# A hybrid decoder block on one core: gates, branch projections and output projection by Strassen's scheme

## The chip, the cores and the metric

The kernel runs on one core of a Trainium2 chip. The metric is device time in microseconds for one execution; the kernel before took 1918.51 us as the median of three runs (1917.52 to 1919.49). A core has a matrix engine (TensorE, PE in the profile, with its weight loads as PEld), a vector engine (VectorE, DVE), an activation engine (ScalarE, ACT), a general engine (GpSimd, POOL) and an engine that here only issues transfers (SyncE, SP). Each engine takes its own queue in order, and waits on semaphores for the others.

## The reference, cut to what matters

One layer works on 1024 tokens and 16 meta tokens in front, with 1024 features. From the normalised stream `xn` one product gives the inputs of three token mixers and the gate logits; each mixer's result is projected, gated and summed, and one more product follows:

```python
xn = rms_norm(x, norm_pre)
proj = xn @ w_in                       # mixers' inputs, and 3 x 1024 gate logits
y_ssd, y_sc, y_dn = three mixers       # each tokens x 1024
branch = einsum("btnw,nwd->btnd", stack([y_ssd, y_sc, y_dn]), w_branch)
gates = sigmoid(gate_logits)           # tokens x 3 x 1024
merged = sum(gates * branch, over the three)
out = merged @ w_out
return x + rms_norm(out, norm_post)    # meta tokens dropped
```

So behind the mixers there are seven products of 1024 x 1024 by 1024 x 1024: three for the gates, three for the branches, one for the output.

## The kernel before

All products are float32 made of three products of rounded parts: a number is split into a high part (ScalarE casts it) and a low part (VectorE subtracts the high part from it), and high times high, high times low and low times high are added up in PSUM (`dense`, L157 to L159). A dense job is 128 output features: its weights come in one 512 KB transfer (`load_raw`, L127), are split (`split`, L135 and L136) one job ahead, and are multiplied with the stream, which stands split in SBUF (`xh`, `xl`), in groups of up to 512 tokens. A matmul of the tail thus has 128 x 128 weights and 512 columns.

The stream is normalised, transposed and split first. Then the mixers run, head by head: eight slots for the DeltaNet heads, eight for pairs of SSD heads. `weave` lays a mixer's small dependent steps between the matmuls of dense jobs: each step says how many columns of dense work it is worth waiting for, times a factor from the table `GAPS`. A DeltaNet slot has eight dense jobs: four of the next head and four of the short-convolution branch. The last SSD slot has three gate jobs (`early_gates`), whose results are parked in DRAM.

Behind the mixers (from `cp` on) the other 21 gate jobs and 24 branch jobs alternate (`gate_job`, `branch_job`). A branch's input is read back from DRAM and split beforehand (`y_tasks`, L974 to L981); the third branch is scaled at that point (L1007). A branch's results are multiplied by the gate straight from PSUM (L1039, L1041) and added to the sum `merged` (L1042). At the end `merged` and `w_out` are split and multiplied token block by token block (L1131 to L1133), and each token block is normalised, scaled, added to x (L1135 to L1149) and stored; the last one in three pieces (L1139, L1144).

The order in each queue is fixed at build time by a scheduler that follows the order of the code and the dependences. GpSimd makes masks and memsets and a few 128x512 sums (L692, L696) while the mixers run, and nothing after them.

Of the kernel before, what the change touches and what calls it, by code (L numbers as in the profile page):

```python
# [83 lines left out]
def hybrid_block(  # L84
# [419 lines left out]
    def dn_mix(h, tiles):  # L504
# [205 lines left out]
    def sc_jobs(t):  # L710
# [170 lines left out]
    def gate_col(b, d):  # L881
        return C_G + b * D + d * P

    def early_gates():
        """The first gates of the branch that comes first, parked in DRAM."""
        for d in range(PARKED):
            def go(w, d=d):
                gs = tmp(f"pg{d}")
                yield from act_job(gs, f"pg{d}", AF.Sigmoid)(w)
                DMA.dma_start(parked[d], gs[:, :SEQ])  # L890

            lazy(gate_col(ORDER[0], d), go)

# [15 lines left out]

    slot("dn", None, lambda: dn_jobs(0, dnt[0]))  # L910
    for h in range(DN_H):
        fs = [lambda h=h: sc_jobs(h)]
# [37 lines left out]
    wk.close()  # L950
    ab.__exit__(None, None, None)

# [1 line left out]
    cp = ctx.enter_context(tc.tile_pool(name="cp", bufs=1))  # L954
    ZERO = [(0, HALF), (HALF, HALF)]
    AHEAD = 3

    def slab(name, dt=F32):
        return cp.tile([P, SEQ], dt, name=name, tag="c", bufs=12)

    merged = [None] * KT
    order = [(b, (y_sd, y_sc, y_dn)[b]) for b in ORDER]
    yt = {}
    gates = {}

    halves = [slice(hf * HALF, (hf + 1) * HALF) for hf in range(2)]

    def staged(src, hi, lo, first=None):
        """Two tasks: fetch half a row block, and put its two exact parts in place."""
        box = {}  # L970

        def fetch():
            box["t"] = cp.tile([P, HALF], F32, tag="yr", name="yr", bufs=3)
            DMA.dma_start(box["t"], src)  # L974

        def put():
            t = box["t"]
            if first is not None:
                first(t)
            A.copy(hi(), t)  # L980
            V.tensor_tensor(lo(), t, hi().bitcast(F32), ALU.subtract)  # L981

        return fetch, put

    def pipelined(pairs, lead=2):
        f, p = [x[0] for x in pairs], [x[1] for x in pairs]
        for i in range(len(pairs) + lead):
            def step(i=i):
                if i >= lead:
                    p[i - lead]()  # L990
                if i < len(pairs):
                    f[i]()
            yield step
# [186 lines left out]
```

## Time and profile before

| | |
|---|---|
| median of the runs | 1918.51 us (1917.52 to 1919.49) |
| span of the profiled execution, first to last instruction | 1917.7 us |
| PE busy | 1892.8 us (99%) |
| DVE busy | 1060.5 us (55%) |
| ACT busy | 688.1 us (36%) |
| POOL busy | 161.8 us (8%) |
| first matmul of the parked gates | 1284.8 us |
| first matmul of the other gates | 1327.1 us |
| first matmul of the output projection | 1822.4 us |
| granted TensorE clock, mean | 0.997 |

The span is 0.8 us below the median of the runs. A row of a timeline gives the start of an instruction in microseconds from the span's start, its duration, engine, line and operation, what it writes and reads, and how long its engine sat idle before it. On PE the next matmul starts before the one in front has ended, so the pace is read from starts or from counts, not from durations.

### The profile page before, as it was taken

How to read it: one execution, taken by the hardware profiler on the slowest of the kernel's cores; microseconds unless marked ns; L12 is line 12 of the kernel's file. 1: busy time of each engine (PE TensorE's matmuls, PEld its weight loads, DVE VectorE, ACT ScalarE, POOL GpSimd, SP SyncE). 2: the span in 40 equal slices, each digit the busy share in tenths (PEclk: the TensorE clock that was granted, in tenths of full speed). 3: DMA queues.
4: the chain of work that ended last, by engine and by line, in shares of the span. 5: the costliest groups of instructions: out<-in, count | busy, mean ns of one | idle time of the engine just before them, and what ended most of it. 6: DMA issues, size and time to landing. Idle time of an engine off the chain costs nothing.

```text
span 1917.7 us, 27827 instructions
## 1 busy us (share of the span) xinstructions
PE 1892.8 (99%) x11475; PEld 1633.1 (85%) x11475; DVE 1060.5 (55%) x1748; ACT 688.1 (36%) x1248; POOL 161.8 (8%) x289
## 2 busy tenths in 40 slices
PE   6999999999999999999999999999999999999998
PEld 5988989889898898988989889888888888888887
DVE  5565666656666566665666788785323223622542
ACT  5543424334243342533425455464312211311231
POOL 2001001010010100101001111110000000000000
PEclk8999999999999999999999999999999999999999
DMA  5211111111211112111122123124413312411312
GB/s 150 58 34 56 44 53 48 45 56 45 62 39 45 56 45 67 34 45 56 45 67 78 56 89 100 56 78 150 130 44 87 100 44 72 135 47 56 116 66 88
DMA packets 163673, 131.40 MB, mean 69 GB/s; under 512 B 9329, under 2 KB 144686, under 8 KB 163546
## 3 DMA queue, kind: packets, MB, share of 16 engines
q1 hardware_dynamic: 162682, 126.74, 22.2%
q8 instruction: 90, 1.47, 0.3%
q10 hardware_dynamic: 720, 2.36, 0.3%
q0 software_dynamic: 144, 0.52, 0.1%
q14 instruction: 37, 0.30, 0.1%
HBM read 111.14 MB, written 18.46 MB: 68 GB/s over the span
## 4 chain that ended last, share of the span: by engine, by line
PE 94%; DVE 3%; ACT 1%; issue 1%; DMA 1%; POOL 0%; SPq 0%; DVEq 0%; POOLq 0%; ACTq 0%
PE b L158 5%; PE b L159 5%; PE b L157 5%; PE g L158 4%; PE g L159 4%; PE g L157 4%; PE po L1132 2%; PE po L1133 2%; PE po L1131 2%; PE pg L157 1%; PE pg L158 1%; PE pg L159 1%; DVE wl L136 0%; DMA gain<-in_norm_pre_dram 0%; PE sm L333 0%
## 5 line engine op out<-in xcount | busy, mean ns | idle before, releaser
L135 ACT CAST wh<-raw 128x1024 fp32r<-128x1024 f32 x132 | 138.7, 1051 | 369.0 <-PE b L158 190.9
L136 DVE TENSOR_TENSOR wl<-raw,wh 128x1024 fp32r<-128x1024 f32 x132 | 162.1, 1228 | 190.8 <-ACT wh L135 190.8
L157 PE MATMUL b<-yh,wh 128*128 128x512 f32 x384 | 149.4, 389 | 0.0
L158 PE MATMUL b<-yl,wh 128*128 128x512 f32 x384 | 149.4, 389 | 0.0
L159 PE MATMUL b<-yh,wl 128*128 128x512 f32 x384 | 149.4, 389 | 0.0
L158 PE MATMUL g<-xl,wh 128*128 128x512 f32 x336 | 133.0, 396 | 0.0
L159 PE MATMUL g<-xh,wl 128*128 128x512 f32 x336 | 132.1, 393 | 0.0
L157 PE MATMUL g<-xh,wh 128*128 128x512 f32 x336 | 132.0, 393 | 0.0
L157 PEld LDWEIGHTS b<-yh,wh 128*128 128x128 f32 x384 | 72.1, 188 | 15.1
L158 PEld LDWEIGHTS b<-yl,wh 128*128 128x128 f32 x384 | 72.1, 188 | 15.0
L159 PEld LDWEIGHTS b<-yh,wl 128*128 128x128 f32 x384 | 72.1, 188 | 15.0
L157 PEld LDWEIGHTS g<-xh,wh 128*128 128x128 f32 x336 | 63.1, 188 | 15.2
L158 PEld LDWEIGHTS g<-xl,wh 128*128 128x128 f32 x336 | 63.0, 188 | 14.7
L159 PEld LDWEIGHTS g<-xh,wl 128*128 128x128 f32 x336 | 63.2, 188 | 14.4
L1041 DVE TENSOR_TENSOR g<-b,g 128x512 f32<-128x512 f32 x32 | 22.1, 691 | 94.6 <-PE b L159 94.6
L1132 PE MATMUL po<-wol,mh 128*128 128x512 f32 (+1 forms) x136 | 51.9, 382 | 0.0
L1131 PE MATMUL po<-woh,mh 128*128 128x512 f32 (+1 forms) x136 | 51.7, 380 | 0.0
L1133 PE MATMUL po<-woh,ml 128*128 128x512 f32 (+1 forms) x136 | 51.4, 381 | 0.0
L981 DVE TENSOR_TENSOR yl<-yr,yh 128x512 fp32r<-128x512 f32 x48 | 32.2, 690 | 32.2 <-ACT yh L980 31.8
L1039 DVE TENSOR_TENSOR mg<-b,g 128x512 f32<-128x512 f32 x16 | 11.1, 692 | 64.8 <-PE b L159 64.8
L1024 ACT ACTIVATE g<-g 128x512 f32<-128x512 f32 x42 | 24.9, 594 | 59.6 <-PE g L159 59.6
L980 ACT CAST yh<-yr 128x512 fp32r<-128x512 f32 x48 | 29.1, 621 | 41.9 <-DMA yr<-y_dn 19.8
(1728 smaller groups left out, 5412.7 us busy)
## 6 DMA issues: line engine op xcount, KB each, us to landing
raw<-in_w_in_dram SPq DMA_DIRECT2D x108, 512.0 KB, 4.0
raw<-in_w_branch_dram SPq DMA_DIRECT2D x24, 512.0 KB, 4.1
yr<-y_dn SPq DMA_DIRECT2D x16, 256.0 KB, 4.4
yr<-y_sc SPq DMA_DIRECT2D x16, 256.0 KB
yr<-y_sd SPq DMA_DIRECT2D x16, 256.0 KB, 3.1
yr<-in_w_out_dram SPq DMA_DIRECT2D x16, 256.0 KB, 4.0
xr<-in_x_dram SPq DMA_DIRECT2D x8, 512.0 KB, 4.2
xt<-in_x_dram SPq DMA_DIRECT2D x7, 512.0 KB, 5.4
```

The costliest lines, as they stand in the source:

```text
L135: A.copy(wh, raws[i])
L136: V.tensor_tensor(wl, raws[i], wh.bitcast(F32), ALU.subtract)
L157: PE.matmul(o, lhsT=wh[:, k, :], rhs=r1, start=k == 0, stop=False)
L158: PE.matmul(o, lhsT=wh[:, k, :], rhs=r2, start=False, stop=False)
L159: PE.matmul(o, lhsT=wl[:, k, :], rhs=r1, start=False, stop=k == KT - 1)
L980: A.copy(hi(), t)
L981: V.tensor_tensor(lo(), t, hi().bitcast(F32), ALU.subtract)
L1024: lambda o, c0, m: A.activation(gs[:, c0 - META:c0 - META + m], o, AF.Sigmoid),
L1041: V.tensor_tensor(gg, o, gg, ALU.mult)
L1131: PE.matmul(ps, lhsT=mh[k][:, tk], rhs=wo["h"][:, k, es], start=k == 0, stop=False)
L1132: PE.matmul(ps, lhsT=mh[k][:, tk], rhs=wo["l"][:, k, es], start=False, stop=False)
L1133: PE.matmul(ps, lhsT=ml[k][:, tk], rhs=wo["h"][:, k, es], start=False, stop=k == KT - 1)
```

## The change

The seven products of the tail are done by Strassen's scheme (in its form with seven products and shared sums). Each operand is cut into four 512 x 512 blocks: a11 to a22 of the weights, b11 to b22 of the tokens. A product of the tail becomes a `Group` of seven block products (`ph` 0 to 6), each with 48 matmuls of 512 columns in four parts (`q`), 16 blocks of 128 x 128 three times over. What enters a block product is a block or a sum of blocks: the sums are made in float32 by GpSimd (`sums_after`, and the t2 of `t_prep`) and by VectorE (s2 in `w_prep`), and each result is then split anew (`t_split`, `w_split`), one product ahead. Two pairs of PSUM banks, y and z, accumulate across products; y is copied out three times (`take_copy`), and a block of the result is a copy plus z (`finish`). In the code `g0` to `g5` are the gates and then the branches, each in the order 2, 1, 0, and the last group is the output.

With that: the stream is written to DRAM near the start (`x_d`: the high part stored from ScalarE's queue, the low part added to it by a GpSimd transfer that accumulates), and read back block by block in each gate group. All gates go to DRAM and are read back. The third branch's input is scaled and written back during the gate groups (`scale_tasks`). The four parked gate jobs' place in the last SSD slot (three jobs) is taken by four short-convolution jobs, so DeltaNet slots have 8, 7, 8, 7, 8, 8, 6 and 8 jobs, with factors 2.3, 2.0 and 1.75 for 8, 7 and 6. The pools of the tail take the memory of the stream's and the mixers' pools, and wait for it tile by tile.

```diff
-GAPS = {"sm": 1.0, "dn": 2.3, "dl": 2.2, "s0": 2.0, "sd": 2.4, "sx": 2.0, "sg": 2.0}
+HK = KT // 2
+GAPS = {"sm": 1.0, 8: 2.3, 7: 2.0, 6: 1.75, "s0": 2.0, "sd": 2.4, "sx": 2.0, "sg": 2.0, "sl": 3.6}
...
+    for h, n in enumerate((4, 3, 4, 3, 4, 4, 2, 4)):
+        fs = [lambda h=h: dn_jobs(h + 1, dnt[h + 1])] if h < DN_H - 1 else [
             lambda: sdg_jobs(0, grps[0]), lambda: sd_jobs(0, sdt[0])]
+        slot(4 + n, lambda h=h: dn_mix(h, dnt[h]), lambda n=n: sc_next(n), *fs)
...
+    for k in range(KT):
+        A.dma_start(x_d[k], xh[:, k, META:].bitcast(F32))
+        GP.dma_start(x_d[k], xl[:, k, META:].bitcast(F32), accum_op=ALU.add)
...
+    def t_split(g, ph, u, src):
+        h = c1.tile([P, 2, HALF], F32R, name=f"th{g.n}_{ph}{u}", tag="th", bufs=4)
+        l = c1.tile([P, 2, HALF], F32R, name=f"tl{g.n}_{ph}{u}", tag="tl", bufs=4)
+        A.copy(h, src)
+        V.tensor_tensor(l, src, h.bitcast(F32), ALU.subtract)
+        g.t[ph, u] = h, l
+    def w_split(g, ph, u, src):
+        h = c1.tile([P, HK, 256], F32R, name=f"wh{g.n}_{ph}{u}", tag="wh", bufs=3)
+        l = c1.tile([P, HK, 256], F32R, name=f"wl{g.n}_{ph}{u}", tag="wl", bufs=3)
+        A.copy(h, src)
+        V.tensor_tensor(l, src, h.bitcast(F32), ALU.subtract)
+        g.w[ph, u] = h, l
+    def both(eng, fn, dst, x, y, op):
+        for u in range(2):
+            eng.tensor_tensor(fn(dst, u), fn(x, u), fn(y, u), op)
...
+        if ph == 2:
+            t2 = g.t2[u] = c2.tile([P, 2, HALF], F32, name=f"t2_{g.n}{u}", tag="t2", bufs=2)
+            GP.tensor_tensor(t2, tk(k["b22"], u), tk(k["b11"], u), SUB)
+            t_split(g, ph, u, t2)
         else:
+            t_split(g, ph, u, tk(k[("b11", "b21", None, "b12", "b11", "b21", "b22")[ph]], u))
...
+            V.tensor_tensor(wk(g.s2, u), wk(k["a22"], u), wk(k["a21"], u), SUB)
+            w_split(g, ph, u, wk(g.s2, u))
+        else:
+            w_split(g, ph, u, wk(k[("a11", "a12", None, "a21", "a11", "a22", "a12")[ph]], u))
+    def sums_after(g, ph):
+        k = g.blk
+        if ph == 0:
+            both(GP, tk, k["b11"], k["b12"], k["b11"], SUB)
+        elif ph == 1:
+            both(GP, tk, k["b12"], k["b22"], k["b12"], SUB)
+        elif ph == 2:
+            for u in range(2):
+                GP.tensor_tensor(tk(k["b21"], u), tk(k["b21"], u), g.t2[u], SUB)
+        elif ph == 3:
+            both(GP, wk, k["a11"], k["a11"], g.s2, ADD)
+        elif ph == 4:
+            both(GP, wk, k["a12"], k["a12"], g.s2, SUB)
+    BANK = "yzyyzyz"
+    def product(g, ph, q):
...
+        for k in range(HK):
+            th, tl = g.t[ph, k // 2]
+            r1, r2 = th[:, k % 2, :], tl[:, k % 2, :]
+            PE.matmul(o, lhsT=wh[:, k, cs], rhs=r1, start=fresh and k == 0, stop=False, skip_group_check=not fresh)
+            PE.matmul(o, lhsT=wh[:, k, cs], rhs=r2, start=False, stop=False, skip_group_check=not fresh)
+            PE.matmul(o, lhsT=wl[:, k, cs], rhs=r1, start=False, stop=k == HK - 1, skip_group_check=not fresh)
...
+    def block_done(g, i, j, u, t, in_psum):
...
+            s = m if first else gt if in_psum else t
+            V.tensor_tensor(s, t, gt, ALU.mult)
+            if not first:
+                V.tensor_tensor(m, m, s, ADD)
...
+    def finish(g, name, u):
...
+        t = g.st.pop((kept_part, u))
...
+        V.tensor_tensor(t, z, t, ADD)
+        block_done(g, int(name[0]) - 1, int(name[1]) - 1, u, t, False)
...
+        for jj in (1 - j, j):
+            es = slice(jj * HALF, (jj + 1) * HALF)
+            o = fin["o", t, jj]
+            V.scalar_tensor_tensor(o, o, tot, fin["x", t][:, es], ALU.mult, ADD)
+            (DMA if jj else A).dma_start(out[t * P:(t + 1) * P, es], o)
```

First place, SyncE's queue (SP) where the mixers end. Before, the last parked gate is followed by the next weights and the first branch's input (`yr`):

```order
L879 DMA rin_d1_98<-sqa4_2_12424 1x512
L127 DMA raw89_13659<-in_w_in_dram 128x8x128
L890 DMA parked2_96<-pg2_13527 128x1024
L127 DMA raw90_13750<-in_w_in_dram 128x8x128
L974 DMA yr_13607<-y_dn0_69 128x512
```

Now the last result of the short convolution (`y_sc7`) stands between the first and the second quarter of block b11:

```order
L883 DMA rin_d1_134<-sqa4_2_12184 1x512
L982 DMA b11__13468<-x_d0_97 128x512
L749 DMA y_sc7_87<-sc7a_13285 128x1024
L982 DMA b11__13468<-x_d1_98 128x512
L982 DMA b11__13468<-x_d2_99 128x512
L982 DMA b11__13468<-x_d3_100 128x512
L987 DMA a11__13473<-in_w_in_dram 128x4x512
```

So what the first block product reads (b11 and a11) is now fetched behind the last dense job of the mixers.

Second place, the vector engine in the second of the three branch groups. Before, the middle of a branch has one split per job and short gate steps:

```order
L136 TENSOR_TENSOR wl113_15249<-raw113_15193,wh113_15248 128x1024
L1041 TENSOR_TENSOR g1_4_14795<-b1_40_15211,g1_4_14795 128x512
L1042 TENSOR_TENSOR mg4_14197<-mg4_14197,g1_4_14795 128x512
L1041 TENSOR_TENSOR g1_4_14795<-b1_41_15238,g1_4_14795 128x512
L1042 TENSOR_TENSOR mg4_14197<-mg4_14197,g1_4_14795 128x512
L136 TENSOR_TENSOR wl114_15309<-raw114_15252,wh114_15308 128x1024
```

Now, between its block products 1 and 3, four splits (tl, wl) for each product, and the finishing of block 11 (L1149 adds z from PSUM, L1131 multiplies by the gate, L1133 adds to `merged`):

```order
L1035 TENSOR_TENSOR tl4_21_15813<-t2_41_15810,th4_21_15812 128x1024
L1149 TENSOR_TENSOR s1_40_15748<-pz_15797,s1_40_15748 128x1024
L1042 TENSOR_TENSOR wl4_21_15851<-s2_4_15830,wh4_21_15850 128x1024
L1131 TENSOR_TENSOR s1_40_15748<-s1_40_15748,g4_000_15787 128x1024
L1133 TENSOR_TENSOR mg00_15342<-mg00_15342,s1_40_15748 128x1024
L1035 TENSOR_TENSOR tl4_30_15867<-b12__15394,th4_30_15866 128x1024
L1042 TENSOR_TENSOR wl4_30_15906<-a21__15399,wh4_30_15905 128x1024
L1035 TENSOR_TENSOR tl4_31_15883<-b12__15394,th4_31_15882 128x1024
L1149 TENSOR_TENSOR s1_41_15785<-pz_15836,s1_41_15785 128x1024
```

GpSimd, which had nothing to do there before, now has in the same group:

```order
L1058 TENSOR_TENSOR t2_40_15791<-b22__15630,b11__15471 128x1024
L1047 TENSOR_TENSOR b12__15394<-b22__15630,b12__15394 128x1024
L1047 TENSOR_TENSOR b11__15471<-b12__15394,b11__15471 128x1024
L1047 TENSOR_TENSOR a11__15476<-a11__15476,s2_4_15830 128x4x256
L1058 TENSOR_TENSOR t2_41_15810<-b22__15630,b11__15471 128x1024
L1047 TENSOR_TENSOR b12__15394<-b22__15630,b12__15394 128x1024
L1047 TENSOR_TENSOR a11__15476<-a11__15476,s2_4_15830 128x4x256
L1082 TENSOR_TENSOR b21__15550<-b21__15550,t2_40_15791 128x1024
```

Both engines now do 128x1024 operations on two SBUF tensors in the same stretch.

Third place, the vector engine's last rows. Before, the last token block ends with:

```order
L1139 TENSOR_TENSOR ot7_17026<-po7_2_17031,gpost_16567 128x256
L1141 RECIPROCAL oss7_17027<-oss7_17027 128x1
L1144 SCALAR_TENSOR_TENSOR ot7_17026<-ot7_17026,oss7_17027,xr7_17024 128x512 x2
```

Now the last split of all, wl6_61, has 44 rows behind it; these are the first four and the last six:

```order
L1042 TENSOR_TENSOR wl6_61_17220<-mg10_15663,wh6_61_17219 128x1024
L1176 TENSOR_TENSOR o100_17252<-py_16784,a11__16777 128x512
L1181 TENSOR_TENSOR oss_16779<-oss_16779 128x1
L1176 TENSOR_TENSOR o100_17252<-py_16784,a11__16777 128x512
...
L1181 TENSOR_TENSOR oss_16779<-oss_16779 128x1
L1187 SCALAR_TENSOR_TENSOR s1_61_16856<-s1_61_16856,oss_16779,b12__17095 128x512
L1187 SCALAR_TENSOR_TENSOR U2_61_17020<-U2_61_17020,oss_16779,b12__17095 128x512
L1183 RECIPROCAL oss_16779<-oss_16779 128x1
L1187 SCALAR_TENSOR_TENSOR s1_61_16856<-s1_61_16856,oss_16779,b12__17095 128x512
L1187 SCALAR_TENSOR_TENSOR U2_61_17020<-U2_61_17020,oss_16779,b12__17095 128x512
```

Of the 44 rows 16 are L1187, eight L1176, four L1146 (the last additions of z), all of 128x512, and 16 are of one column. All eight token blocks are finished in these rows.

## Rows read from the trace of the kernel before

**Rows 1.** The page: engine, busy us (share of the span), instructions.

```profile
PE 1892.8 (99%) x11475; PEld 1633.1 (85%) x11475; DVE 1060.5 (55%) x1748; ACT 688.1 (36%) x1248; POOL 161.8 (8%) x289
```

**Rows 2.** Groups by line on PE, 1284 to 1917 us: count, busy, mean ns.

```profile
L157 PE MATMUL b<-yh,wh 128*128 128x512 f32 x384 | 149.4, 389 | 0.0
...
L157 PE MATMUL g<-xh,wh 128*128 128x512 f32 x336 | 132.0, 393 | 0.0
...
L1131 PE MATMUL po<-woh,mh 128*128 128x512 f32 x120 | 47.2, 393 | 0.0
...
L157 PE MATMUL pg<-xh,wh 128*128 128x512 f32 x48 | 19.7, 411 | 0.0
```

**Rows 3.** Stretches, PE alone: stretch, us, busy (matmuls), clock, DMA share, GB/s.

```profile
1330.00:1370.00 40.00, 40.00 (x175) 1.00 0.72 227
1782.00:1820.00 38.00, 38.00 (x169) 1.00 0.46 146
1824.00:1902.00 78.00, 78.00 (x337) 1.00 0.24 81
```

**Rows 4.** Groups by line on DVE, 1327 to 1917 us.

```profile
L136 DVE TENSOR_TENSOR wl<-raw,wh 128x1024 fp32r<-128x1024 f32 x44 | 53.8, 1223 | 134.4 <-ACT wh L135 134.4
...
L1042 DVE TENSOR_TENSOR mg<-mg,g 128x512 f32<-128x512 f32 x32 | 22.1, 692 | 1.0
...
L1007 DVE SCALAR_TENSOR_TENSOR yr<-yr,snw,rin 128x512 f32<-128x512 f32 x16 | 11.8, 749 | 6.9 <-DMA yr<-y_sd 4.3 <-DMA rin<-rin_d 2.5
...
L1137 DVE TENSOR_TENSOR oss<-oss 128x1 f32<-128x1 f32 x9 | 1.4, 160 | 52.6 <-ACT oj L1135 52.6
```

**Rows 5.** Groups by line on ACT, 1327 to 1917 us.

```profile
L135 ACT CAST wh<-raw 128x1024 fp32r<-128x1024 f32 x44 | 46.3, 1052 | 261.5 <-PE b L158 190.9 <-PE g L158 61.9 <-PE pg L158 4.7
```

**Rows 6.** Timeline of POOL, 182 to 204 us.

```profile
182.38 2.27 POOL L692 TENSOR_TENSOR dm0osq<-dm0osq,dn0q 128x512 f32<-128x512 f32 x1 [5.26 <-ACT dm0osq L691]
...
200.02 1.29 POOL L692 TENSOR_TENSOR dm0osq<-dm0osq,dn0q 128x512 f32<-128x512 f32 x1 [13.15 <-ACT dm0osq L691]
```

**Rows 7.** Timeline of DVE, 182 to 186 us.

```profile
182.22 1.28 DVE L437 SCALAR_TENSOR_TENSOR dn1q<-dn1qraw,cols,dn1q 128x1024 f32<-128x1024 f32 x1
...
183.67 2.06 DVE L437 SCALAR_TENSOR_TENSOR dn1q<-dn1qraw,cols,dn1q 128x1024 f32<-128x1024 f32 x1
```

**Rows 8.** Timeline of DVE, 1033 to 1037 us.

```profile
1033.59 1.21 DVE L136 TENSOR_TENSOR wl<-raw,wh 128x1024 fp32r<-128x1024 f32 x1
1034.73 2.33 DVE L437 SCALAR_TENSOR_TENSOR sd0x<-sd0xraw,cols,sd0x 128x1040 f32<-128x1040 f32 x1
```

**Rows 9.** Timeline of POOL, 1033 to 1037 us.

```profile
1033.85 2.11 POOL L696 TENSOR_TENSOR dm7ol<-dm7osq,dm7oh 128x512 fp32r<-128x512 f32 x1 [0.74 <-ACT dm7oh L694]
```

**Rows 10.** Timeline of POOL: a select alone, and one beside a busy DVE.

```profile
232.88 0.64 POOL L561 TENSOR_SCALAR_AFFINE_SELECT dm1An<-dm1An 128x512 f32<-128x512 f32 x1 [5.99 <-DVE dm1An L559]
...
1180.90 4.59 POOL L467 TENSOR_SCALAR_AFFINE_SELECT sm4F<-sm4F 128x512 f32<-128x512 f32 x1 [11.18 <-DVE sm4F L465]
```

**Rows 11.** Stretches, all engines: PE, PEld, DVE, ACT, POOL busy, clock, DMA, GB/s.

```profile
16.00:20.00 4.00, 1.91 (x8) 1.33 (x9) 3.09 (x5) 2.45 (x4) 0.00 (x0) 0.62 1.09 386
20.00:24.00 4.00, 4.00 (x16) 3.39 (x15) 3.91 (x9) 3.35 (x8) 0.00 (x0) 0.53 1.13 326
...
1335.00:1340.00 5.00, 5.00 (x23) 4.06 (x22) 1.39 (x2) 2.23 (x4) 0.00 (x0) 1.00 1.03 410
```

**Rows 12.** Timeline of the last microseconds, 1911.4 to 1917.7 us.

```profile
1911.47 0.28 PE L1133 MATMUL po<-woh,ml 128*128 128x256 f32 x1
...
1914.53 0.34 ACTq L1145 DMA_DIRECT2D out_dram<-ot  x1
```

**Rows 13.** Timeline of all engines, 249 to 250.2 us, inside a DeltaNet slot.

```profile
249.16 0.38 ACT L615 CAST dm1Z<-dm1z 128x256 f16<-128x256 f32 x1 [0.55 <-PE dm1z L610]
...
250.01 0.17 PE L626 MATMUL dm1u<-dm1Z,dm1XU 16*16 16x8 f16 x1
```

**Rows 14.** Stretch of one DeltaNet slot, all engines.

```profile
179.00:298.00 119.00, 118.62 (x840) 104.83 (x839) 73.41 (x127) 44.38 (x95) 13.90 (x26) 1.00 0.17 50
```

More of the change, by code (lines that the diff above doesn't have):

```diff
@@ L879, in sd_mix @@
                 DMA.dma_start(rin_d[t // 4][:, b.outs], sqa[b][0:1, :])
[L881 to L892, printed above, removed]
     dnt = [{} for _ in range(DN_H)]
@@ L949, in hybrid_block @@
         weave(mix() if callable(mix) else mix, n, GAPS[kind])
[L950 to L993, printed above, removed]
@@ new lines, in hybrid_block, with tk, wk @@
+    groups = [Group(n, kind, b) for n, (kind, b) in enumerate(ORDER_C)]
+    def tk(t, u):
+        return t[:, 2 * u:2 * u + 2, :]
+    def wk(t, u):
+        return t[:, :, u * 256:(u + 1) * 256]
+    def t_split(g, ph, u, src):
[4 more added lines that the diff above has]
+        g.t[ph, u] = h, l
@@ new lines, in take_copy, with gates_in @@
+    def take_copy(g, ph, u):
+        n = {0: "s1", 2: "U2", 3: "U3"}.get(ph)
+        if n:
+            t = g.st[n, u] = state(f"{n}_{g.n}{u}")
+            A.copy(t, g.ps["y", u])
+    def gates_in(g, i, j):
+        if g.kind == "b":
+            for u in range(2):
+                t = g.gt[i, j, u] = slab(f"g{g.n}_{i}{j}{u}")
+                DMA.dma_start(t, gate_d[g.b, i, j, u])
+    def block_done(g, i, j, u, t, in_psum):
+        if g.kind == "g":
+            s = slab(f"sg{g.n}_{i}{j}{u}") if in_psum else t
+            A.activation(s, t, AF.Sigmoid)
+            A.dma_start(gate_d[g.b, i, j, u], s)
+        elif g.kind == "b":
+            gt = g.gt.pop((i, j, u))
+            first = g.b == ORDER[0]
+            if first and (i, j) not in merged:
+                merged[i, j] = c2.tile([P, HK, HALF], F32, name=f"mg{i}{j}", tag=f"mg{i}{j}")
+            m = merged[i, j][:, 2 * u:2 * u + 2, :]
+            s = m if first else gt if in_psum else t
+            V.tensor_tensor(s, t, gt, ALU.mult)
+            if not first:
+                V.tensor_tensor(m, m, s, ADD)
+        else:
+            out_quarter(g, i, j, u, t, in_psum)
@@ new lines, in hybrid_block, with out_setup, residual @@
+    fin = {}
+    def out_setup():
+        gp = block("a11")
+        fin["gpost"] = gp.rearrange("p k f -> p (k f)")[:, 0:D]
+        DMA.dma_start(fin["gpost"], norm_post.broadcast_to([P, D]))
+        fin["ss"] = c2.tile([P, SEQ // P, 4], F32, name="oss", tag="oss")
+    def residual(tag, t0):
+        xr = block(tag).rearrange("p k f -> p (k f)")
+        for v in range(2):
+            t = t0 + v
+            fin["x", t] = xr[:, v * D:(v + 1) * D]
+            DMA.dma_start(fin["x", t], x[t * P:(t + 1) * P, :])
@@ new lines, in hybrid_block @@
+    extra = scale_tasks()
+    for g in groups:
+        g.ps, g.st, g.gt, g.t2 = {}, {}, {}, {}
+    last = len(groups) - 1
+    g0 = groups[0]
+    g0.load("b11", "a11")
+    for u in range(2):
+        t_prep(g0, 0, u)
+        w_prep(g0, 0, u)
+    g0.load("b21", "a12", "b12", "a21", "b22", "a22")
+    both(GP, wk, g0.blk["a21"], g0.blk["a11"], g0.blk["a21"], SUB)
+    for g in groups:
+        nxt = groups[g.n + 1] if g.n < last else None
+        prev = groups[g.n - 1] if g.n else None
+        for ph in range(7):
+            pg, pp = (g, ph + 1) if ph < 6 else (nxt, 0)
+            if nxt is not None:
+                nxt.load(*{3: ("b12", "a21"), 4: ("b11", "a11"), 5: ("b21", "a22"), 6: ("b22", "a12")}.get(ph, ()))
+            gates_in(g, *{1: (0, 0), 4: (1, 1), 5: (1, 0), 6: (0, 1)}[ph]) if ph in (1, 4, 5, 6) else None
+            if g.kind == "o":
+                if ph == 0:
+                    out_setup()
+                if ph == 1:
+                    both(V, wk, g.blk["a21"], g.blk["a11"], g.blk["a21"], SUB)
+                if ph in (1, 2, 3):
+                    residual(("a12", "a21", "a22")[ph - 1], 2 * (ph + 1) % 8)
+                elif ph == 4:
+                    residual("b12", 2)
+            for q in range(PAIRS):
+                if pg is not None:
+                    if q < 2:
+                        t_prep(pg, pp, q)
+                    else:
+                        w_prep(pg, pp, q - 2)
+                if q == 1:
+                    sums_after(g, ph)
+                    if ph == 6 and nxt is not None and nxt.kind != "o":
+                        both(GP, wk, nxt.blk["a21"], nxt.blk["a11"], nxt.blk["a21"], SUB)
+                if q % 2:
+                    u = q // 2
+                    if ph == 0 and prev is not None:
+                        finish(prev, "12", u)
+                    elif ph == 2:
+                        finish(g, "11", u)
+                    elif ph == 5:
+                        finish(g, "22", u)
+                    elif ph == 6:
+                        finish(g, "21", u)
+                    if g.n in (1, 2) and extra:
+                        extra.pop(0)()
+                product(g, ph, q)
+                if q % 2:
+                    take_copy(g, ph, q // 2)
@@ L1154 @@
+    for u in range(2):
+        finish(groups[last], "12", u)
 _INS = ["x", "meta_tokens", "norm_pre", "norm_post", "w_in", "ssd_conv_w", "ssd_conv_b", "ssd_dt_bias", "ssd_a_log",
```

293 lines of the change are left out of this document (140 added, 153 removed).

## The prediction

> **What bounds the kernel now.** I read the page first: PE is busy 99% of the span [rows 1], VectorE 55%, GpSimd 8%. So a term counts only if it takes matmuls away or makes PE wait. Second come the groups by line in the tail [rows 2]. The reader is to see the counts there: L157, L158 and L159 each have as many, so gates have 3 x 336 + 3 x 48 = 1152 matmuls, branches 3 x 384 = 1152, the output 3 x 120 of 512 columns. Third, the pace. A stretch holds the matmuls that start in it and the one that began before, 0.39 us long; so gates come every 40.39/175 = 0.2308 us, branches every 38.39/169 = 0.2272 us, the output every 78.39/337 = 0.2326 us, all at a granted clock of 1.00 (the 2.4 GHz level) [rows 3]. The tail has no stall to win back: what can shrink it is fewer matmuls.
>
> **What it removes.** 1152 x 0.2308 + 1152 x 0.2272 + 360 x 0.2326 = 265.9 + 261.7 + 83.7 us, and 5.5 us for the last token block's 48 matmuls of 256 columns at half a pace: 616.9 us. **What it adds on PE**: 7 groups x 7 products x 48 = 2352 matmuls of 512 columns. Their moving operand lies like the branches' (512 columns at the start of a dense row), so I take 0.2272: 534.4 us. That is 82.5 us less; by the gates' pace 542.8, 74.1 less. One group is 336 x 0.2272 = 76.3 us, one product 10.9 us.
>
> **The hand-over.** Before, PE goes from one gate job to the next without a pause. Now the first block product needs b11 and a11, whose place in SBUF is the stream's, and on SP the last short-convolution result stands ahead of three quarters of b11 and of a11. That result waits for the last dense matmul and a 128x512 VectorE step, 0.69 us [rows 4]. Then five issues at 0.34 us [rows 12], so a11 leaves some 2.7 us behind PE's last matmul. y_sc7, b11 and a11 are 2.25 MB; at the best rate seen, 410 GB/s [rows 11], 5.5 us, and the last store of the span takes 2.8 us from the end of its issue to the end [rows 12], which I take as the fixed part. a11 lands near 8.6 us, its cast takes 1.05 us [rows 5]: PE is idle about 9.7 us. Behind a start with pauses the granted clock was 0.62 and 0.53 for 8 us [rows 11], near the 1.2 GHz level, with PE fully busy in the second half; I add 3 us for that. 13 us; ends 8 (data early, clock kept) and 20 (326 GB/s, the clock low for 8 us).
>
> **The sums and splits, on VectorE and GpSimd.** This is the term that decides. In a group VectorE makes 28 splits and 2 sums (s2) of 128x1024 from two SBUF tensors, 1.22 us each [rows 4]: 36.6 us. GpSimd makes 14 sums of 128x1024. The trace has it only with 512 columns: 1.29 us alone [rows 6], so 2.58 us for 1024, 36.1 us a group. By themselves both fit in 76.3 us. But the trace shows them excluding each other. At 182.38 GpSimd's sum starts beside a VectorE step on two SBUF tensors that ends at 183.50; it takes 2.27 us, 0.98 more than alone [rows 6, 7]. The next VectorE step of that kind starts at 183.67, inside it, and takes 2.06 us where its twin takes 1.28: it ends as if it had begun when GpSimd ended. The same at 1033.85: the sum started inside a VectorE split and took 2.11 us, and the step behind that split 2.33 us [rows 8, 9]. So I add the two.
> - Gate groups g1 and g2: 36.6 + 36.1 = 72.7 us of 76.3. Fits; 1 us each for an uneven spread, since eight of the 14 sums belong to the last product of the group before and the first two.
> - g0 also takes the scaling of the third branch, 16 steps of 0.75 us [rows 4]: 84.7, so 8.4 over.
> - The first branch group multiplies six results from SBUF by gates from SBUF (6 x 1.22): 80.0, 3.7 over.
> - The other two also add eight times into `merged`: 14 x 1.22 more, 89.8 us, 13.5 over each.
> - Output: 12 sums, 32 steps of 1.22 and 8 of 0.69: 75.5. 1 us.
> Sum 2 + 8.4 + 3.7 + 27 + 1 = 42 us. Against this, VectorE's steps start 0.08 us before the one in front has ended [rows 8], so back to back they cost 1.14; and 1024 columns may cost less than twice 512. With 1.14 and 2.4 the second branch group is 83.8, 7.5 over, and the whole 18 us. I take 33 us, nearer to the durations as they stand. The ends are 0 (the exclusion doesn't hold PE up) and 106 (below).
>
> The Trainium skill, page "SBUF — State Buffer", section "Who interferes with whom", says that a VectorE instruction with two SBUF inputs and a GpSimd instruction that reads SBUF share a port as an exclusive lock, so that the later one waits for the whole of the other. By that rule these sums are added, as I do; the trace agrees at both places. By the page "GPSIMD Engine Reference", section "Elementwise — side-by-side cycle accounting", 2048 elements take 4497 ns; between that and the 1.29 us of the trace an estimate for 1024 is 2.36 us, which would make the term some 15 us smaller.
>
> ScalarE in a gate group: 28 casts, 6 copies and 8 sigmoids of that size at 1.05 us and eight issues at 0.34 [rows 5, 12], 47 us of 76: hidden. Transfers: 8.4 MB in and 4.2 MB of gates in 76 us, 165 GB/s of 410 [rows 11]: hidden, once g0 runs.
>
> **The end.** Now 5.9 us lie between PE's last matmul (1911.75) and the span's end [rows 12]. After, VectorE has 44 rows behind the last split: 12 of 0.69, 16 of 0.75 and 16 of 0.16 [rows 4], 22.9 us, less 44 x 0.08: 19.4 us, and some 2 for answers from ScalarE. The last split is wanted at the middle of the last product, 5.5 us before PE ends, and can be done at its start, 10.9 before. So VectorE ends 10.5 to 16 us behind PE, and the store takes 3.1: 16 us in the middle, 10 more than now (ends 7 and 14).
>
> **Mixers and start.** The three parked gate jobs are in the counts above. Three DeltaNet slots lose one, one and two jobs, and their factors fall from 2.3 to 2.0 and 1.75. A step that asked for 2000 columns got 4600 (1.92 us), now 3500 (1.46) at the least. In a doubling step ScalarE's cast ends at 249.54 and PE takes it up at 250.01, 0.47 us later [rows 13]: just eaten by 1.75. I take 2 us for waits. The store of the stream puts eight issues on ScalarE near 45 us, eight on GpSimd: 1 us, since 12 MB at 326 to 410 GB/s [rows 11] pass beside weights fetched two jobs ahead. 3 us; ends 0 and 15.
>
> **Sum.** 1917.7 - 82.5 + 13 + 33 + 10 + 3 = 1894.2 us of span; the median of the runs is 0.8 above the span: **1895 us**.
>
> **Rivals.**
> 1. The exclusion is hidden. VectorE is four splits ahead per product and the sums one product ahead; the light products (3 and 4 of a group have only splits) could take up what the heavy ones leave. For it: g1 and g2 fit. Against it: in the later branch groups the sum is over the 76.3 us, which no order mends. The 33 us go: 1862 us.
> 2. Slower: GpSimd is kept off the port. A select that takes 0.64 us alone took 4.59 at 1180.90, while VectorE ran step after step [rows 10]: it waited 3.95 us, through three steps and not one. If each of the 14 sums waits so, GpSimd needs 14 x 6.53 = 91.4 us a group, 15.1 over, and the block products 2 and 3 wait for their sums in all seven groups: 106 us in place of 33, 1968 us. It decides from a mean wait of 3.45 us per sum on (56.5 us in all, no gain left). Against it: at 182 and 1033 GpSimd came in behind one step.
> 3. Also slower: the mixers' chains. A DeltaNet slot is 119 us with 8 jobs [rows 14], one job 72 matmuls or some 10.9 us. If the three shortened slots don't shrink, four jobs' worth is lost, 44 us, in place of 2: 1937 us. Against it: the same steps ran at 99.7% PE there, and most steps have more slack than the one above.
>
> **How the numbers follow.** Forecast 0.55 (1878 to 1914 for itself), rival 1 0.25, rival 2 0.12, rival 3 0.08. The range reaches down to rival 1 and up past no change, leaving out rival 2's price and the worse half of rival 3: 1852 to 1932. A run can be told from no change at about 0.2%, 3.8 us. Faster: rival 1 and 0.52 of the forecast, 0.77; within 0.2%: 0.04; slower: the rest with rivals 2 and 3, 0.19.
>
> **What would show it.** Right: 2352 matmuls of the products at 0.227 us where nothing waits; an idle stretch of PE of about 10 us where the mixers end, and a lower granted clock behind it; GpSimd's sums at 2.5 us alone and up to 3.8 beside splits, splits of up to 3.8; the gaps of PE mostly in g0 and the second and third branch groups, ended by ScalarE's casts or VectorE's splits; VectorE alone busy in the last 12 us. Wrong: branch groups of 76 us with no gaps (rival 1); sums of over 6 us and PE waiting for t2 in every group (rival 2); PE gaps inside DeltaNet slots 2, 4 and 7 (rival 3). Splits that keep 1.22 us beside running sums would take the ground from the term itself.

## The result, and the profile after

The changed kernel takes 1933.13 us (median, 1932.76 to 1934.95), the kernel before 1918.75 us: a ratio of 1.0077, 95% interval 1.0062 to 1.0091. It is slower by 14.4 us; 1895 us was predicted, faster.

The profiled execution has a span of 1931.6 us. The first part of its page answers to [rows 1]:

```profile
PE 1835.5 (95%) x11115; PEld 1580.9 (82%) x11115; DVE 1380.2 (71%) x1842; ACT 825.7 (43%) x1341; POOL 474.2 (25%) x393
```

PE has 360 instructions less, as counted, but it is no longer busy 99% of the span. VectorE grew by 320 us, GpSimd by 312 us. Next the stretches of the new stage: the pause behind the mixers' last matmul, the seven groups from first matmul to first matmul, and what follows PE's last one. Columns as in [rows 11]; the first number behind the stretch is its length.

```profile
1300.11:1311.83 11.72, 0.00 (x1) 0.00 (x0) 3.16 (x4) 3.18 (x4) 0.00 (x0) 0.72 0.90 307
1311.83:1415.07 103.24, 84.04 (x336) 66.94 (x337) 72.83 (x56) 43.90 (x45) 57.12 (x20) 0.88 0.70 260
1415.07:1494.91 79.84, 76.75 (x337) 62.91 (x336) 61.87 (x36) 40.50 (x42) 42.36 (x15) 1.00 0.45 152
1494.91:1576.21 81.30, 77.08 (x338) 62.83 (x336) 64.45 (x37) 41.38 (x43) 43.15 (x15) 1.00 0.50 169
1576.21:1656.93 80.72, 78.16 (x337) 63.96 (x336) 70.35 (x44) 35.71 (x37) 42.85 (x14) 0.98 0.48 162
1656.93:1740.83 83.90, 79.73 (x337) 64.76 (x336) 77.15 (x51) 34.24 (x35) 43.41 (x14) 0.96 0.42 145
1740.83:1827.97 87.14, 79.17 (x337) 64.06 (x336) 82.29 (x51) 33.99 (x34) 50.83 (x14) 0.96 0.42 139
1827.97:1920.52 92.55, 81.09 (x337) 65.08 (x335) 78.97 (x73) 40.93 (x63) 29.16 (x10) 0.93 0.10 35
1920.52:1931.60 11.08, 0.00 (x0) 0.00 (x0) 7.64 (x18) 2.33 (x7) 0.00 (x0) 0.61 0.51 189
```

Undisturbed, a group is 336 x 0.2272 = 76.3 us, and no group keeps to it. They are over by 26.9, 3.5, 5.0, 4.4, 7.6, 10.8 and 16.2 us: 74 us, of which 2 are the low clock behind the pause. PE's waits from the mixers' end to its last matmul (us in total, times, longest):

```profile
PE py L1101 <- ACT wh L1041: 20.5, 2, 11.7
PE py L1103 <- DVE wl L1042: 17.7, 6, 8.7
PE py L1102 <- DVE tl L1035: 12.5, 6, 3.5
PE pz L1103 <- DVE wl L1042: 8.1, 3, 6.1
PE py L1101 <- ACT U L1110: 3.4, 2, 1.7
PE pz L1102 <- DVE tl L1035: 2.1, 2, 1.9
```

The 11.7 us is the hand-over. All others come to 52.6 us, and most end with a split on VectorE. In groups 2 to 6 they all stand at the third and fourth product, but for one of 1.3 us.

Why the splits are late is seen by laying the two timelines side by side. The first fence is VectorE in the second group, the second GpSimd (start, us):

```profile
1429.84 3.43 DVE L1035 TENSOR_TENSOR tl<-t,th 128x1024 fp32r<-128x1024 f32 x1
1433.19 3.41 DVE L1042 TENSOR_TENSOR wl<-s,wh 128x1024 fp32r<-128x1024 f32 x1
1436.52 3.41 DVE L1035 TENSOR_TENSOR tl<-t,th 128x1024 fp32r<-128x1024 f32 x1
1439.85 1.21 DVE L1149 TENSOR_TENSOR s<-pz,s 128x1024 f32<-128x1024 f32 x1
```

```profile
1328.65 2.40 POOL L1058 TENSOR_TENSOR t<-b__13505,b__13468 128x1024 f32<-128x1024 f32 x1
...
1428.79 3.39 POOL L1082 TENSOR_TENSOR b__13889<-b__13889,t 128x1024 f32<-128x1024 f32 x1
1432.13 3.38 POOL L1047 TENSOR_TENSOR a__13971<-a__13971,s 128x1024 f32<-128x1024 f32 x1
1435.47 3.37 POOL L1082 TENSOR_TENSOR b__13889<-b__13889,t 128x1024 f32<-128x1024 f32 x1
1438.80 3.39 POOL L1047 TENSOR_TENSOR a__13971<-a__13971,s 128x1024 f32<-128x1024 f32 x1
```

A sum takes 2.40 us while VectorE is idle (1328.65). Here the two engines take strict turns: each record begins inside the other engine's and lasts until its own turn is done, 3.35 us for one sum and one split. A split that takes 1.22 us by itself takes 3.41. The step at 1439.85, which reads one input from PSUM, is not held off: 1.21 us, inside a sum. Beside the split rows of [rows 4], VectorE's groups in the new stage (mean ns) read:

```profile
L1035 DVE TENSOR_TENSOR tl<-t,th 128x1024 fp32r<-128x1024 f32 x14 | 43.2, 3083 | 13.8 <-ACT th L1034 13.8
L1042 DVE TENSOR_TENSOR wl<-s,wh 128x1024 fp32r<-128x1024 f32 x14 | 39.6, 2836 | 0.0
L1149 DVE TENSOR_TENSOR U<-pz,U 128x1024 f32<-128x1024 f32 x26 | 31.6, 1217 | 10.3 <-PE pz L1103 10.3
```

And the sums don't run where the code puts them. Twelve of the second group's stand in one row on GpSimd, from 1404.10 to 1442.2: the last six, for a11, b21 and a12, are wanted only by products 5 to 7, yet run as soon as their inputs are there. In these 38 us VectorE gets one two-input step per 3.35 us, and PE multiplies three and a half products, each with four splits.

The first group differs. There VectorE also sits idle, 10.4 and 3.3 us, for the casts of the two t2, and ScalarE for GpSimd's sums: here the sums themselves come late.

```profile
1331.08 1.05 ACT L1034 CAST th<-t 128x1024 fp32r<-128x1024 f32 x1 [5.11 <-POOL t L1058]
1332.17 2.32 DVE L1035 TENSOR_TENSOR tl<-t,th 128x1024 fp32r<-128x1024 f32 x1 [10.43 <-ACT th L1034]
1336.75 1.04 ACT L1034 CAST th<-t 128x1024 fp32r<-128x1024 f32 x1 [4.62 <-POOL t L1058]
1337.83 2.27 DVE L1035 TENSOR_TENSOR tl<-t,th 128x1024 fp32r<-128x1024 f32 x1 [3.34 <-ACT th L1034]
```

### The profile page after: what moved, and what is told of

Read it like the earlier page. It is cut to its first block, busy times and chain, and to the rows that moved or that the text cites. A ratio compares the mean times of both kernels' runs of the same rounds, so it can differ in the third digit from the quotient of the medians.

```text
span 1931.6 us, 27668 instructions
## 1 busy us (share of the span) xinstructions
PE 1835.5 (95%) x11115; PEld 1580.9 (82%) x11115; DVE 1380.2 (71%) x1842; ACT 825.7 (43%) x1341; POOL 474.2 (25%) x393
## 4 chain that ended last, share of the span: by engine, by line
PE 75%; DVE 12%; issue 5%; DMA 3%; POOL 3%; ACT 2%; SPq 0%; DVEq 0%; ACTq 0%; POOLq 0%
DVE tl L1035 3%; PE py L1103 3%; PE py L1102 3%; DVE wl L1042 3%; PE py L1101 3%; PE pz L1103 2%; PE pz L1102 2%; PE pz L1101 2%; POOL t L1058 1%; DMA a__13894<-in_w_in_dram 1%; DVE s L1068 1%; DMA b__13498<-x_d 0%; DVE U L1149 0%; POOL b__16016 L1047 0%; DMA gain<-in_norm_pre_dram 0%
## 5 line engine op out<-in xcount | busy, mean ns | idle before, releaser
L1101 PE MATMUL py<-th,wh 128*128 128x512 f32 x448 | 179.2, 400 | 23.9 <-ACT wh L1041 20.5
L1103 PE MATMUL py<-th,wl 128*128 128x512 f32 x448 | 179.6, 401 | 17.8 <-DVE wl L1042 17.7
L1102 PE MATMUL py<-tl,wh 128*128 128x512 f32 x448 | 179.7, 401 | 12.5 <-DVE tl L1035 12.5
L1103 PE MATMUL pz<-th,wl 128*128 128x512 f32 x336 | 133.0, 396 | 8.1 <-DVE wl L1042 8.1
L1102 PE MATMUL pz<-tl,wh 128*128 128x512 f32 x336 | 132.6, 395 | 2.1 <-DVE tl L1035 2.1
L1101 PE MATMUL pz<-th,wh 128*128 128x512 f32 x336 | 132.5, 394 | 0.0
L1101 PEld LDWEIGHTS py<-th,wh 128*128 128x128 f32 x448 | 86.8, 194 | 43.5 <-ACT wh L1041 21.3
L1103 PEld LDWEIGHTS py<-th,wl 128*128 128x128 f32 x448 | 86.8, 194 | 40.1 <-DVE wl L1042 22.1
L1102 PEld LDWEIGHTS py<-tl,wh 128*128 128x128 f32 x448 | 86.9, 194 | 33.2 <-DVE tl L1035 15.1
L1103 PEld LDWEIGHTS pz<-th,wl 128*128 128x128 f32 x336 | 64.2, 191 | 23.2 <-DVE wl L1042 9.9
L1035 DVE TENSOR_TENSOR tl<-t,th 128x1024 fp32r<-128x1024 f32 x14 | 43.2, 3083 | 13.8 <-ACT th L1034 13.8
L1149 DVE TENSOR_TENSOR U<-pz,U 128x1024 f32<-128x1024 f32 x26 | 31.6, 1217 | 10.3 <-PE pz L1103 10.3
```

Of the source, the lines that this page charges most:

```text
L1035: V.tensor_tensor(l, src, h.bitcast(F32), ALU.subtract)
L1101: PE.matmul(o, lhsT=wh[:, k, cs], rhs=r1, start=fresh and k == 0, stop=False, skip_group_check=not fresh)
L1102: PE.matmul(o, lhsT=wh[:, k, cs], rhs=r2, start=False, stop=False, skip_group_check=not fresh)
L1103: PE.matmul(o, lhsT=wl[:, k, cs], rhs=r1, start=False, stop=k == HK - 1, skip_group_check=not fresh)
L1149: V.tensor_tensor(t, z, t, ADD)
```

## The experiments

**e1, without the sums.** The edit, with the two a21 sums and t2 taken out in the same way:

```
 def sums_after(g, ph):
-    k = g.blk
-    if ph == 0:
-        both(GP, tk, k["b11"], k["b12"], k["b11"], SUB)
-    ...
+    return
```

> All GpSimd sums of the seven groups are left out: the splits read blocks that hold no sums, so the products are of other numbers; 2352 matmuls, all splits, VectorE's two sums per group and all finishing steps stay. In the changed kernel the matmul stage takes 608.6 us for 534.4 us of matmuls, 74.2 us over: 2.0 the clock behind the hand-over, 15.6 at the second to fourth product of the first group, 9.1 at its last product (VectorE waits for a transfer of a22), 12.8 at products 3 and 4 of groups 2 to 4, 18.4 there in groups 5 and 6, 16.1 in the output group. Theory A (each running sum holds VectorE's two-input steps off, 2.3 us a sum): the stalls at products 2 to 4 go, 15.6 + 12.8 + 18.4 + 16.1 = 63 us: 1870 us, between 1863 and 1888. Rival B (VectorE and ScalarE need that long for their own steps, or wait for PE's results in a ring): the stalls stay, 1915 us or more. In both the 9.1 us of a22 may stay.

1862.4 us (1860.9 to 1864.4), ratio to the kernel before 0.971 [0.9695, 0.9724]. All but the hand-over is gone, the wait for a22 as well (1.1 us left), so the time lies just below theory A's range. The stretches are the second and the fifth group:

```profile
1391.03:1467.18 76.15, 76.15 (x337) 63.10 (x336) 42.49 (x37) 42.06 (x43) 0.00 (x0) 1.00 0.48 166
1619.51:1695.66 76.15, 76.15 (x337) 63.09 (x336) 58.37 (x51) 34.26 (x35) 0.00 (x0) 1.00 0.46 159
```

VectorE's own steps need 42.5 us in a gate group; with the sums running nearly the same count took 61.9. This falls in with theory A and against B, but it leaves open whether the sums cost by holding VectorE off or by coming late to those who wait for them. e2 and e6 tell these apart.

**e2, the sums on VectorE.** All eight places of this form, nothing left out:

```
-            both(GP, tk, k["b11"], k["b12"], k["b11"], SUB)
+            both(V, tk, k["b11"], k["b12"], k["b11"], SUB)
```

> All sums on VectorE in place of GpSimd, nothing left out. Theory A (exclusion): a sum costs VectorE 1.14 us in place of the 2.3 us it is held off, so the twelve sums of the first products take 14 us of VectorE's time and not 28, and the stalls shrink to some 10 us in all, above all in the fifth and sixth group, whose 64 VectorE steps need 73 of 76 us: 1880 us, between 1868 and 1895. Rival B (own steps or a ring with PE bound it): VectorE gets 14 steps per group more, 16 us, and the time rises above 1945 us.

1860.85 us (1860.08 to 1861.12), ratio 0.9701 [0.9685, 0.9717]: faster than either kernel, 72 us below the changed one, and below what theory A named. PE's waits in the new stage, and the second and fifth group:

```profile
PE py L1101 <- ACT wh L1041: 12.6, 3, 11.8
```

```profile
1411.07:1487.23 76.16, 76.16 (x337) 63.08 (x336) 62.13 (x55) 43.67 (x44) 0.00 (x0) 1.00 0.51 180
1639.55:1715.71 76.16, 76.16 (x337) 63.08 (x336) 70.55 (x63) 34.16 (x34) 0.00 (x0) 1.00 0.49 166
```

VectorE does 14 steps more per group and is busy no longer than in the changed kernel (62.1 us beside 61.9). Even at 70.6 of 76.2 us PE never waits for it; I had left it 10 us of stalls.

**e3, the sums on GpSimd, spread out.** The last six of a group wait for the last matmul of a product's first quarter, as here (`paced` is `both` with that wait):

```
+    def after_pe(ins):
+        tc.add_manual_dep(ins.ins, PE_LAST[-1].name, ...)
 ...
         elif ph == 2:
-            for u in range(2):
-                GP.tensor_tensor(tk(k["b21"], u), tk(k["b21"], u), g.t2[u], SUB)
+            paced(GP, wk, k["a11"], k["a11"], g.s2, ADD)
         elif ph == 3:
+            for u in range(2):
+                after_pe(GP.tensor_tensor(tk(k["b21"], u), tk(k["b21"], u), g.t2[u], SUB))
```

> The sums stay on GpSimd, but the last six of a group's fourteen wait for PE: a11's for the first quarter of product 3, b21's of product 4, a12's of product 5, where the changed kernel runs twelve in a row beside products 1 to 3. Theory C (the bunch decides: VectorE does one step per 3.35 us for 40 us, and needs 18 steps in that time): the stalls at products 3 and 4 go in groups 2 to 4 (12.8 us) and shrink by half in groups 5 to 7 (17 us), 1903 us, between 1895 and 1915. Theory D (the group's total decides, as the prediction's sum has it: both engines' time added against 76.3 us): the order of sums changes nothing within 5 us, 1928 to 1938 us.

1918.9 us, ten runs between 1909.2 and 1924.0, ratio 0.9999 [0.9986, 1.0013]. Neither theory is right alone. The second and the fifth group:

```profile
1414.81:1490.97 76.16, 76.16 (x337) 63.06 (x336) 60.23 (x36) 41.33 (x42) 42.56 (x15) 1.00 0.48 164
1643.97:1731.13 87.16, 80.19 (x337) 64.82 (x336) 81.41 (x50) 33.96 (x35) 52.23 (x15) 0.96 0.44 150
```

Groups 2 to 4 run without a stall (76.2, 76.2 and 76.8 us in place of 79.8, 81.3 and 80.7), with the same work on both engines: there the row of twelve was the whole cause, theory C. Groups 5 to 7 take 87.2, 88.9 and 88.4 us in place of 83.9, 87.1 and 92.6: the fifth and sixth got longer. Theory D explains a part of that. By e1's count VectorE has 58.4 us of its own in the fifth group, and 14 sums at 2.40 us are 33.6. Less eight steps of 1.22 us that read PSUM and can stand beside a sum, that is 82 us, 6 over, where 10.8 were lost. In the output group the same count gives 76 us (47.0 by e1's trace, and twelve sums), which would fit. What makes up the rest is not shown. e3 leaves the first six sums of a group in one row, and the sixth group's whole loss stands at its second product, behind that row (1727.93 to 1750.13 us); a run with these spread too would tell.

```profile
1747.85 3.35 DVE L1035 TENSOR_TENSOR tl<-b__16092,th 128x1024 fp32r<-128x1024 f32 x1
1752.40 0.80 PE L1113 MATMUL pz<-th,wl 128*128 128x512 f32 x1 [6.91 <-DVE wl L1042]
```

The first group hardly gained (101.8 us).

**e4, s2 behind the split**, in the queue's order alone:

```
+            s = V.tensor_tensor(wk(g.s2, u), wk(k["a22"], u), wk(k["a21"], u), SUB)
+            if g.n:
+                tc.add_manual_dep(s.ins, LAST_WL[g.n - 1].name, ...)
```

> One edit: VectorE's sum s2 of the next group is queued behind the last split of the group in front. In the changed kernel it stands ahead of the splits of a12 and waits 8.9 us for the transfer of a22, which can only start when the split of the a22 before has read its place. Theory E (that queue place costs PE 9.1 us at the first group's last product): 1924 us, between 1920 and 1928. Rival F (s2 is wanted then: the wait shows up again at the second group's third product): no change within 3 us of 1933.

1933.6 us, ratio to the kernel before 1.0081 [1.0066, 1.0096]: nothing gained, rival F. The first fence is VectorE's s2 in the changed kernel, the second the same step in e4, the third e4's second group:

```profile
1398.26 2.36 DVE L1068 TENSOR_TENSOR s<-a__13894,a__13742 128x1024 f32<-128x1024 f32 x2 [8.92 <-DMA a__13894<-in_w_in_dram]
```

```profile
1399.89 2.36 DVE L1070 TENSOR_TENSOR s<-a__13894,a__13742 128x1024 f32<-128x1024 f32 x2 [2.34 <-DMA a__13894<-in_w_in_dram]
```

```profile
1407.12:1495.29 88.17, 81.20 (x338) 64.94 (x337) 70.44 (x39) 42.53 (x44) 50.80 (x17) 0.96 0.42 144
```

The stall at the first group's last product is gone, and the second group lost 11.8 us in place of 3.5: the two splits done first fell beside GpSimd's a21 sum, so that s2 ends no sooner, and the row of twelve begins where it did (1403.46 us; 1404.10 in the changed kernel). PE alone is 8 us earlier (1407.1 and 1415.1), and meets that row with so much less lead. A stall taken out in front of a bottleneck comes back at it.

**e5, the first loads in the order of use**, on top of e2:

```
-    g0.load("b11", "a11")
+    for u in range(2):
+        for k in (2 * u, 2 * u + 1):
+            DMA.dma_start(g0.blk["b11"][:, k, :], x_d[k][:, 0:HALF])
+        ...
+        DMA.dma_start(wk(g0.blk["a11"], u), w_in[0:HALF, c:c + 256].rearrange("(k p) f -> p k f", p=P))
```

> The sums on VectorE as in e2, and the first group's first two blocks are fetched in the order of use: b11's first two rows of tiles, the first half of a11's columns, b11's other two, the other half (in e2: four tiles of b11, then a11 as one transfer of 1 MB). In e2 PE stands idle 11.8 us between the mixers' last matmul and the first product, and the last transfer it waits for is a11, 7.5 us from issue to landing. Theory G (the 2.25 MB ahead of the first matmul set the pause): 1.5 MB stand ahead of it now, at 300 to 400 GB/s 2 to 3 us less, a part of it given back at the wait for the other half of b11: 1858 us, between 1856.5 and 1860.5. Rival H (the fixed parts decide: the store of the last result, the issues, the landing): no change, 1860 to 1862.

1862.4 us (1861.5 to 1864.2), ratio 0.971 [0.9697, 0.9723], no gain over e2. The first matmul of the new stage in e2, and in e5:

```profile
1309.67 0.80 PE L1101 MATMUL py<-th,wh 128*128 128x512 f32 x1 [11.81 <-ACT wh L1041]
```

```profile
1308.30 0.80 PE L1101 MATMUL py<-th,wh 128*128 128x512 f32 x1 [8.72 <-ACT wh L1041]
```

The pause did shrink by 3.1 us, as theory G has it, but the first group took 82.9 us in place of 79.6: 3.2 us given back at waits for the other halves and at the low clock. The time is H's to within 0.4 us, the reason isn't.

**e6, sums that nobody wants**, on top of e2: four per product, each behind a matmul and on a tile of its own.

```
+    def idle_sums():
+        for _ in range(4):
+            s = GP.tensor_tensor(scr, scr, scr, ADD)
+            tc.add_manual_dep(s.ins, PE_LAST[-1].name, ...)
```

> The sums on VectorE as in e2, and 196 sums of 128x512 on GpSimd added that read and write one tile of their own: four per product, each four behind a matmul of it, and no instruction waits for them. They are as much work as the 98 sums of 128x1024 of the changed kernel (1.29 us each alone). Theory A (a running GpSimd sum holds off VectorE's steps with two inputs in SBUF, whoever wants its result): VectorE's steps stretch to 2 us and more, and the groups lose time as if the sums were added: gate groups some 7 to 14 us, the two later branch groups 22 to 31, the first group and the output 10 to 24: 1970 us, between 1910 and 2000. Rival I (the changed kernel lost its time because GpSimd's sums came late to those who wanted them): 1861 us, within 4.

1943.3 us (1940.5 to 1947.1), ratio 1.013 [1.0116, 1.0144]: 82 us slower than e2, and no instruction waits for GpSimd. (The changed kernel has 96 sums, not 98.) Second and fifth group, and the output group:

```profile
1401.38:1488.25 86.87, 80.50 (x338) 64.74 (x336) 78.22 (x56) 41.14 (x42) 52.81 (x28) 0.96 0.48 170
1652.17:1742.27 90.10, 80.33 (x337) 63.60 (x336) 86.41 (x62) 34.33 (x34) 54.14 (x28) 0.98 0.41 138
1824.97:1926.16 101.19, 84.89 (x337) 67.14 (x335) 96.60 (x79) 38.77 (x58) 59.43 (x37) 0.88 0.06 21
```

VectorE makes as many steps as in e2 (56 beside 55, 62 beside 63) in 16 us more. So the running of the sums costs by itself, with as much work at least what the changed kernel lost (82 beside 72 us): theory A, and rival I falls. The time is 27 us below the one named: the two later branch groups lost 13.8 and 6.4 us, not 22 to 31. In the sixth it was GpSimd that was held up: from 1750.7 us on, 23 of its sums took 80.5 us, 3.5 us each. And e6 doesn't show that lateness costs nothing: in the changed kernel's first group it had a part.

## Why the prediction was wrong

The sum of the prediction, term by term, against the changed kernel's trace (us):

| term | predicted | measured |
|---|---|---|
| matmuls removed and added | -82.5 | -82.5 at the predicted 10.91 us for 48 matmuls; they took 10.88 where nothing waits, 1.3 us less in all |
| hand-over, with its clock | 13 | 11.7 + 2.0 |
| sums and splits on VectorE and GpSimd | 33 | 72 |
| end | 10 | 5.2: 11.1 behind PE's last matmul in place of 5.9 |
| mixers and start | 3 | 5.1, what is left of the difference of the spans |

**The step that failed** is the size of the port term, 72 us where 33 were taken: "Fits; 1 us each for an uneven spread". The mechanism, VectorE held off by running sums, was right (e6; in the first group late sums come on top), and so was the price, if a little high: one sum and one split take 3.35 us together, where 1.22 + 2.58 = 3.80 was assumed. (The estimate of 2.36 us for such a sum, from the Trainium skill, page "GPSIMD Engine Reference", section "Elementwise — side-by-side cycle accounting", is close to the 2.40 that the trace shows alone. It would have made the term smaller still, by the prediction's own sums some 12 us and not the 15 that it names.) Wrong was to hold the two engines' totals against the 76.3 us of a group. A total says only that a group cannot be shorter. Within it the sums stand in one row, because GpSimd does each as soon as its inputs allow and nothing holds it back, and for that row VectorE falls behind PE by more than its lead of one product. e3 shows one part: with the row broken up the gate and first branch groups fit, as the totals said. The later branch groups then lose 10.8 and 12.6 us; that this is near the 13.5 each of the totals is in part luck, since by the measured prices the totals are only some 6 us over.

By place the 42 us (of which I took 33) and the 72 us differ like this. Groups 2 to 4: 5.7 predicted, 12.9 measured, the row (e3). Groups 5 and 6: 27 predicted, 18.4 measured, of which the totals at the measured prices give some 12. Output: 1 predicted, 16.2 measured. Its s2, a21 and a12 are made of `merged`, which is complete only when VectorE has finished the last branch group, so its sums and steps crowd into its first three products; with all of them on VectorE it loses 0.8 us (77.1 us in e2). First group: 8.4 predicted, 24.9 measured; the scaling was counted, but not that its blocks arrive while product 1 runs, so that the sums come late. GpSimd's seven sums up to the second t2 follow at 2.4 us and more, behind them two s2 at 3.3 us each, and PE waits 8.8 and 4.2 us for the third product's splits. How much of this is lateness and how much the port was not separated. Its 9.1 us at the last product, s2 in front of a split, are of the kind that comes back elsewhere when taken away (e4), and go with the sums (e1).

**A second step was missing**: the clock. I priced it at the hand-over alone. Here is PE at the first group's third product (start, us):

```profile
1344.57 0.80 PE L1101 MATMUL py<-th,wh 128*128 128x512 f32 x1 [8.77 <-ACT wh L1041]
1345.16 0.63 PE L1102 MATMUL py<-tl,wh 128*128 128x512 f32 x1
1350.03 0.79 PE L1103 MATMUL py<-th,wl 128*128 128x512 f32 x1 [4.24 <-DVE wl L1042]
```

The granted clock is 0.50 in this stretch, the 1.2 GHz level:

```profile
1344.57:1352.75 8.18, 3.94 (x8) 2.64 (x9) 8.18 (x4) 5.93 (x6) 8.18 (x4) 0.50 0.16 64
```

Matmuls start 0.43 us apart there in place of 0.23. 72 matmuls of the stage last over 0.55 us, each 0.2 us more from start to start: some 14 us, of which 1.4 at the hand-over. With the waits of 52.6 us that makes some 65 of the 72 us; the rest, a few tenths at each wait and small differences in pace, is not broken down.

**The rivals.** Rival 1 named 1862 us for a term of nothing; e1 gives 1862.4 and e2 1860.9, so the rest of the sum holds, with a term too long (the end) and one too short (mixers) that nearly cancel. Rival 2 is what the time came nearest to in kind, a block product waiting for sums, but not in its mechanism: a sum takes 3.25 us in the mean and 2.40 alone, a wait of 0.85 us, not 3.45. Rival 3 fell: the shortened slots shrank, and the mixers ended near 1300 us.

**The end** was put 5 us too long: VectorE had 18 rows left behind PE's last matmul, not the whole 44; the first token blocks are finished beside PE. **The hand-over** came out as worked out in sum (13.7 us for 13), with some luck: PE was idle 11.7 us in place of 9.7, and the low clock cost 2.0 us in place of 3. The mixers' end is not known better than 3 us: in the seven profiles of kernels with the same mixers, the changed one's and the experiments', their last matmul ends between 1297.9 and 1301.3. (The prediction's 1.92 and 1.46 us for 4600 and 3500 columns are 2.07 and 1.58 by the gates' pace of [rows 3]; nothing else rests on them.)

## What to carry to other kernels

Work moved to GpSimd to relieve VectorE is not beside it where both read two inputs from SBUF: price each sum at its own 2.4 us of VectorE's time, and move it only if VectorE would need longer for it (here 1.14). Compare totals per stage for a lower bound, then look at where the steps stand in each queue: an engine that nothing holds back does its work in one row, and that row, not the average, is what the waiting engine sees. Price the low clock behind every stall, not only the planned one.

## What was not expected of the hardware

GpSimd can also be shut out altogether. VectorE at 1737 us runs two-input steps 1.14 us apart and none is stretched; the sum that starts at 1738.66 takes 10.14 us:

```profile
1738.66 10.14 POOL L1058 TENSOR_TENSOR t<-b__16170,b__16016 128x1024 f32<-128x1024 f32 x1
```

```profile
1745.30 1.22 DVE L1042 TENSOR_TENSOR wl<-a__16172,wh 128x1024 fp32r<-128x1024 f32 x1
1746.44 1.22 DVE L1149 TENSOR_TENSOR U<-pz,U 128x1024 f32<-128x1024 f32 x1
1747.68 2.19 DVE L1131 TENSOR_TENSOR U<-U,g 128x1024 f32<-128x1024 f32 x1
```

It ends at 1748.80, 2.36 us behind the start of the step that reads PSUM, as if it had got in there, after waiting through seven two-input steps. From then on the two take turns at 3.35 us. What decides between being shut out and taking turns was not tried. The Trainium skill, page "SBUF — State Buffer", section "Who interferes with whom", says that a VectorE instruction with at most one SBUF input, outside its two-port modes, does not contend with GpSimd; the steps that read PSUM agree, 1217 ns in the mean in the changed kernel and 1218 in e2. And e3 spread over 15 us in ten runs, where the others kept within 7 in four or five. Taking turns alone doesn't explain it: the changed kernel, whose engines do so too, kept within 2.2 us.
